# A hybrid decoder block: transposes between column halves in its last stage, and attention's output turned by an fp32 product

## The chip, the cores and the metric

The kernel runs on one core of one Trainium2 chip. The metric is the device time of one execution in microseconds (us). Three runs of the kernel before the change gave 1221.88, 1227.33 and 1224.06 us, with a median of 1224.06 us.

## The reference

One decoder layer on 1024 tokens of 1024 features, all in fp32:

```
hn  = RMSNorm(x)
z   = hn @ w_in                  # q | k | v | forget logits | pool input
A   = causal softmax attention, 8 heads of 64, logits += c[t] - c[s], c = cumsum(log sigmoid(f))
B   = multi-scale causal means of the pool input, minus the token, per-group linear
h   = x + RMSNorm(concat(RMSNorm(A), RMSNorm(B)) @ w_out)
h   = h + RMSNorm(SwiGLU(RMSNorm(h)))        # 1024 -> 2816 -> 1024
out = h + sigmoid(h @ w_ple_gate) * RMSNorm(p @ w_ple_proj)
```

## The kernel before, in words

A product of fp32 precision is made of three products of reduced fp32 (`mm3`, lines 111 to 113): each operand is split into a high part (a cast on ScalarE, line 105) and a low part (a subtraction on VectorE, line 106), and hi·hi, hi·lo and lo·hi are added up in PSUM. Tokens come in 8 tiles of 128, features in 8 blocks of 128. `transposed` (line 121) turns a tile by TensorE transposes against an identity, four to a PSUM bank, and splits what it turned.

The program is written as straight loops, and a planner orders each engine's instructions ahead of time by its own estimate of when each becomes ready, the earlier in the program text the more urgent. Each engine then works through its list strictly in that order; an instruction that waits holds up all behind it. `issue_after(ins)` puts what is written under it behind `ins` on that engine. DMAs are issued from the SP queue, except where named.

The stages: (1) the embedding of p, the norm of x, v and forget logits; (2) the pool mixer, with `pool_in` and `pool_out`; (3) q and k, by `qk_pair`, which for a pair of heads computes q and k as 2 x 2 products of 24 matmuls of 512 columns (`project`), splits each into `qk_hi` (ScalarE, line 409) and `qk_lo` (VectorE, line 410), and writes both to `qd` and `kd` in HBM. `qk_hi` and `qk_lo` have one buffer each; (4) attention, one `head(h)` after another, which reads `qs`, `kh`, `kl`, `vh` and `ncb` back from HBM, and for each of four groups of two query tiles makes scores, softmax (line 439), turned probabilities, and the product with v into bank `O` (lines 469, 470). Since v is held as hi beside lo, that product has 128 rows: 64 from v's high part and 64 from its low part. It is copied to `ot` (line 472), turned by two TensorE transposes (line 475), and the two parts are added: a copy on ScalarE (478), an addition on VectorE (479), and the scaling by 1/sum on GpSimd (480); (5) output projection, SwiGLU and the down projection; (6) the last stage, the gate of the p embedding.

PSUM has 8 banks, dealt out by tags. `psum_layout` deals them anew: before `head(0)`, from A=3, F=2, T=2, O=1 to A=2, T=3, O=2, F=1. `qk_pair(0)` and `qk_pair(1)` use the tags A and F of the old layout in turn, five banks; `qk_pair(2)` and `qk_pair(3)` use F of the new one, a single bank, between the heads' matmuls.

In the last stage, `hidden(t)` loads h1 and the embedding of token tile t (`he`), computes the row norm of `acc` (line 98 on ScalarE, 91 and 93 on GpSimd), scales it (`dn`, line 1002), adds it to h1 (line 1003, on GpSimd for all tiles but the first), and turns and splits it (`h3`, line 121 for all tiles but the first; the first is turned in the down stage, line 1048). `gated(t)` multiplies it with the gate's weights in two halves of 512 columns (banks A and F, 24 matmuls each), applies the sigmoid (line 1066), the product and the sum (1067, 1068), and writes out. `hidden(t + 1)` stands ahead of `gated(t)` in the program.

Of the kernel before, what the change touches and what calls it, by code (L numbers as in the profile page):

```python
# [8 lines left out]
F32 = mybir.dt.float32  # L9
F32R = mybir.dt.float32r  # L10
BF16 = mybir.dt.bfloat16
AF = mybir.ActivationFunctionType
# [24 lines left out]
def block_kernel(ctx: ExitStack, tc: tile.TileContext, x, p, g_mix_pre, w_in, b_forget, g_attn_grp,  # L37
# [8 lines left out]
    def pool(stack, name, bufs=1, side=None):  # L46
        return stack.enter_context(tc.tile_pool(name=name, bufs=bufs, side=side, reuse_waits="tile"))
# [21 lines left out]
    make_identity(nc, ident)  # L69
    identb = const.tile([P, P], BF16, name="identb")  # L70
    nc.vector.tensor_copy(identb, ident)
    maskf = const.tile([P, P], BF16, name="maskf")
    nc.gpsimd.memset(maskf, 0.0)
    nc.gpsimd.affine_select(out=maskf, in_=maskf, compare_op=ALU.is_ge, fill=NEG, base=0,
# [49 lines left out]
    def tok(t):  # L124
        return slice(t * P, (t + 1) * P)
# [317 lines left out]
    def head(h):  # L443
        qs = st.tile([P, S], F32R, name="qs")
        nc.sync.dma_start(out=qs.bitcast(F32), in_=qd[h])
        kh = st.tile([P, S], F32R, name="kh")
        kl = st.tile([P, S], F32R, name="kl")
        for j in range(2):
            nc.sync.dma_start(out=kh[j * DH:(j + 1) * DH, :].bitcast(F32), in_=kd[h][0:DH, :])
            nc.sync.dma_start(out=kl[j * DH:(j + 1) * DH, :].bitcast(F32), in_=kd[h][DH:P, :])  # L450
        vh = st.tile([P, NT, P], F32R, name="vh")
        nc.sync.dma_start(out=vh.bitcast(F32), in_=vd[h])
        ncb = st.tile([P, S], F32, name="ncb")
        nc.sync.dma_start(out=ncb, in_=cd[h:h + 1, :].partition_broadcast(P))
        for g in range(NT // 2):
            nj = 2 * g + 2
            pTs = [pt_.tile([P, NT, W2], F32R, name=f"pT{i}") for i in range(2)]
            rsum = sp.tile([P, 2], F32, name="rsum")
            for qi in range(2):
                i = 2 * g + qi  # L460
                s_sb = scores(h, i, qs, kh, kl, ncb, rsum[:, qi:qi + 1])
                cols = slice(qi * P, (qi + 1) * P)
                transposed(s_sb, pTs[0][:, :, cols], pTs[1][:, :, cols], i + 1, "T")
            rinv = sp.tile([P, 2], F32, name="rinv")
            nc.vector.reciprocal(rinv, rsum)
            po = bank("O")
            for j in range(nj):
                q0 = max(0, j - 2 * g) * P
                nc.tensor.matmul(po[:, q0:W2], vh[:, j, :], pTs[0][:, j, q0:W2], start=j == 0, stop=False)
                nc.tensor.matmul(po[:, q0:W2], vh[:, j, :], pTs[1][:, j, q0:W2], start=False, stop=j == nj - 1)  # L470
            ot = sp.tile([P, W2], F32, name="ot", bufs=2)
            nc.scalar.copy(ot, po[:, 0:W2])
            pr = bank("O")
            for qi in range(2):
                nc.tensor.transpose(pr[:, tok(qi)], ot[:, tok(qi)], ident)
            oh = sp.tile([P, 2, DH], F32, name="oh", bufs=2)
            pv = pr[:, 0:W2].rearrange("a (j x d) -> a j x d", x=2, d=DH)
            nc.scalar.copy(oh, pv[:, :, 0, :])
            nc.vector.tensor_tensor(out=oh, in0=oh, in1=pv[:, :, 1, :], op=ALU.add)
            nc.gpsimd.tensor_tensor(out=a_sb[:, 2 * g:2 * g + 2, h * DH:(h + 1) * DH], in0=oh,  # L480
                                    in1=rinv.unsqueeze(2).broadcast_to([P, 2, DH]), op=ALU.mult)

    qk_pair(0, "AF")
    qk_pair(1, "AF")
    psum_layout(A=2, T=3, O=2, F=1)
    head(0)
    head(1)
    qk_pair(2, "F")
    head(2)
# [10 lines left out]
    def wide(name, dt=F32, shape=(2, D)):  # L500

        return wg.tile([P, *shape], dt, name=name, tag="wide", bufs=2)
# [425 lines left out]
    with ExitStack() as c1:  # L928
        fds = [pool(c1, f"fd{i}", side="right") for i in range(3)]
        acc = pool(c1, "accp").tile([P, NT, D], F32, name="acc")  # L930
        gfp = pool(c1, "gfpp").tile([P, D], F32, name="gfp")
        sgp = pool(c1, "sgp", 6)
        rawp = [pool(c1, f"rawp{i}", 8) for i in range(2)]

# [56 lines left out]
            split(raw, wpg[k][0], wpg[k][1])  # L993

        def hidden(t):
            he = wide("he")
            ht, et = he[:, 0, :], he[:, 1, :]
            nc.sync.dma_start(out=ht, in_=h1d[tok(t), :])
            nc.sync.dma_start(out=et, in_=ed[tok(t), :])
            dn = narrow("dn")  # L1000
            r = row_rstd(acc[:, t, :], D, "y")
            nc.vector.scalar_tensor_tensor(out=dn, in0=acc[:, t, :], scalar=r, in1=gfp, op0=ALU.mult, op1=ALU.mult)  # L1002
            (nc.gpsimd if t else nc.vector).tensor_tensor(out=ht, in0=ht, in1=dn, op=ALU.add)  # L1003
            h3 = [fds[t % 3].tile([P, KT, P], F32R, name=f"h3{i}", tag="lr"[i]) for i in range(2)]
            if t:
                transposed(ht, h3[0], h3[1], KT, "T")
            return ht, et, h3

        LAST = len(steps) - 1
        WPG_AT = {LAST - 13: 0, LAST - 11: 1, LAST - 9: 2, LAST - 8: 3, LAST - 7: 4, LAST - 4: 5, LAST - 3: 6, LAST - 2: 7}  # L1010
# [6 lines left out]
        for j, (ci, i, u) in enumerate(steps):  # L1017
            if j + 2 <= LAST:
                prepare(j + 2)
            if j == LAST // 2:  # L1020
                nc.sync.dma_start(out=gfp, in_=g_ffn_post[0:1, :].partition_broadcast(P))
            if j in WPG_AT:
                with tc.issue_after(last_load[0]):
                    load_wpg(WPG_AT[j])
            name, kind, outs = SUMS[i]
            (l, r), which = made.pop((name, u)), (ci + (kind > 0)) % 2
            fresh, begins, ends = i in (0, 1, 5), u == CHUNKS[ci][0], u == CHUNKS[ci][-1]
            if fresh and begins:
                sets[which] = [down_ps.tile([P, 2, HALF], F32, name=f"dp{which}{x}") for x in range(2)]
            for t in range(4):  # L1030
                pv = sets[which][t // 2]
                for k in range(len(u)):
                    for x, (a_, b_) in enumerate(((0, 0), (0, 1), (1, 0))):
                        nc.tensor.matmul(pv[:, t % 2, :], l[:, a_, k, tok(t)], r[:, b_, k, :],  # L1034
                                         start=fresh and begins and k == 0 and x == 0,
                                         stop=ends and k == len(u) - 1 and x == 2, skip_group_check=not fresh)
                if ends and t % 2 == 1:
                    for sh, dh in outs:
                        av = acc[:, 4 * sh + t - 1:4 * sh + t + 1, half(dh)]
                        if (sh, dh, t) in touched:  # L1040
                            nc.vector.tensor_tensor(out=av, in0=pv, in1=av, op=ALU.add)
                        else:
                            nc.scalar.copy(av, pv)
                            touched.add((sh, dh, t))
                if j == LAST and t == 1:
                    tp = down_ps.tile([P, 2, HALF], F32, name=f"dp{1 - which}0").rearrange("a n (j b) -> a (n j) b", b=P)
                    for c in range(KT):
                        nc.tensor.transpose(tp[:, c, :], prev[0][:, c * P:(c + 1) * P], ident)
                    split(tp, prev[2][0], prev[2][1])
            if j == LAST - 2:  # L1050
                with tc.issue_after(last_load[0]):
                    prev = hidden(0)
# [2 lines left out]
        for tag in "TFOA":  # L1055
            bank(tag)

        def gated(t, ht, et, h3):
            for c0, c1_, tag in ((0, 512, "A"), (512, 1024, "F")) if t < NT - 1 else ((0, 512, "A"), (512, 768, "F"), (768, 1024, "A")):
                cols, n = slice(c0, c1_), c1_ - c0  # L1060
                ps = bank(tag)[:, 0:n]
                for k in range(KT):
                    mm3(ps, (h3[0][:, k, :], h3[1][:, k, :]), (wpg[k][0][:, cols], wpg[k][1][:, cols]),
                        k == 0, k == KT - 1)
                sg = sgp.tile([P, HALF], F32, name="sgm")[:, 0:n]
                nc.scalar.activation(out=sg, in_=ps, func=AF.Sigmoid)  # L1066
                nc.vector.tensor_tensor(out=sg, in0=sg, in1=et[:, cols], op=ALU.mult)  # L1067
                nc.vector.tensor_tensor(out=ht[:, cols], in0=ht[:, cols], in1=sg, op=ALU.add)  # L1068
                nc.sync.dma_start(out=out[tok(t), cols], in_=ht[:, cols])

        for t in range(NT):
            nxt = hidden(t + 1) if t + 1 < NT else None
            gated(t, *prev)
            prev = nxt
    banks["ctx"].close()
    f_ctx.close()

# [25 lines left out]
```

## Time and profile before

| | |
|---|---|
| median of three runs | 1224.06 us |
| the profiled execution: its time, its span | 1219.11 us, 1217.3 us |
| granted TensorE clock, mean | 0.997 |
| PE / DVE / ACT / POOL busy, share of the span | 97% / 61% / 44% / 19% |

PE is TensorE's matmul queue, PEld its weight loads, DVE VectorE, ACT ScalarE, POOL GpSimd, SP the queue that issues DMAs. A busy PE is not a PE at its peak, since a matmul's record runs from start to its modelled end, and neighbours overlap. What sets the pace is the distance from one start to the next.

### The profile page before, as it was taken

Reading aid. Unit: us, or ns where it says so; the run is one execution under the profiler, and the core shown is the slowest. Engines: PE = TensorE matmul, PEld = TensorE weight load, DVE = VectorE, ACT = ScalarE, POOL = GpSimd, SP = SyncE. Lnnn points to the kernel's source line nnn. Section 1 sums busy time; section 2 is a strip of 40 time slices with the busy share of each in tenths; the row PEclk is TensorE's granted clock in tenths of the full one; section 3 lists DMA queues with packets and bytes.
Section 4 is the critical chain, followed back from the end, with each engine's and each line's share of the span. In section 5 each row is a group of like instructions: output and inputs, shape, how many; then the busy total and the mean of one; then the engine's idle time right before and its main releaser. Section 6 shows DMA issues by size and latency. Waiting matters only on the chain. (4 is left out here: it accounts for less than half of the span.)

```text
span 1217.3 us, 15811 instructions
## 1 busy us (share of the span) xinstructions
PE 1181.7 (97%) x5832; PEld 978.4 (80%) x5832; DVE 742.3 (61%) x1129; ACT 538.7 (44%) x990; POOL 229.7 (19%) x277
## 2 busy tenths in 40 slices
PE   8999998999999999899999999999999999998998
PEld 6998887887887887688888888888877888887777
DVE  6544834557775568865555456554576967976323
ACT  6433534557875554633333333334245433544111
POOL 2110110000002530242323233232210000004120
PEclk9999999999999999999999999999999999999999
DMA  9732485549831443232332323323266363442332
GB/s 300 238 105 62 138 241 179 152 122 277 241 89 53 156 141 120 97 111 96 121 113 80 110 96 121 101 82 122 98 221 219 106 240 102 157 168 83 114 137 87
DMA packets 110989, 170.19 MB, mean 140 GB/s; under 512 B 9408, under 2 KB 64512, under 8 KB 110912
## 3 DMA queue, kind: packets, MB, share of 16 engines
q1 hardware_dynamic: 110352, 167.35, 42.3%
q0 software_dynamic: 560, 1.84, 0.4%
q8 instruction: 46, 0.75, 0.2%
q14 instruction: 31, 0.25, 0.1%
HBM read 119.58 MB, written 49.58 MB: 139 GB/s over the span
## 5 line engine op out<-in xcount | busy, mean ns | idle before, releaser
L1034 PE MATMUL dp<-r,l 128*128 128x512 f32 x924 | 211.9, 390 | 3.2 <-DVE l L106 2.5
L1034 PEld LDWEIGHTS dp<-r,l 128*128 128x128 f32 x924 | 172.8, 188 | 41.7 <-DVE l L106 4.7
L621 POOL TENSOR_TENSOR w_raw<-w_raw 128x512 f32<-128x512 f32 x80 | 118.0, 1478 | 285.3 <-DMA w_raw<-in_w_ffn_gate_dram 117.2
L106 DVE TENSOR_TENSOR wr<-w_raw,wr 128x512 fp32r<-128x512 f32 x88 | 65.2, 743 | 72.8 <-ACT wr L105 72.4
L106 DVE TENSOR_TENSOR wl<-w_raw,wl 128x512 fp32r<-128x512 f32 x62 | 55.6, 914 | 47.7 <-ACT wl L105 47.7
L105 ACT CAST wr<-w_raw 128x512 fp32r<-128x512 f32 x88 | 54.4, 620 | 62.9 <-PE ps_O L645 14.5
L105 ACT CAST l<-l 128x1024 fp32r<-128x1024 f32 (+1 forms) x42 | 41.1, 980 | 82.7 <-DMA l<-fa_S 46.5
L645 PE MATMUL ps_F<-T,wr 128*128 128x512 f32 x300 | 73.3, 391 | 1.8 <-ACT wr L105 1.0
L645 PEld LDWEIGHTS ps_F<-T,wr 128*128 128x128 f32 x300 | 56.2, 188 | 14.7 <-ACT wr L105 1.4
L645 PE MATMUL ps_A<-T,wr 128*128 128x512 f32 x264 | 64.3, 390 | 0.0
L106 DVE TENSOR_TENSOR l<-l 128x1024 fp32r<-128x1024 f32 (+1 forms) x42 | 47.4, 1133 | 25.2 <-ACT l L105 25.0
L106 DVE TENSOR_TENSOR pT<-ps_T,pT 128x512 fp32r<-128x512 f32 (+2 forms) x96 | 51.1, 552 | 18.8 <-ACT pT L105 18.1
L645 PE MATMUL ps_O<-T,wr 128*128 128x512 f32 x252 | 62.3, 391 | 0.0
L645 PE MATMUL ps_T<-T,wr 128*128 128x512 f32 x240 | 59.7, 391 | 1.1 <-ACT wr L105 1.1
L645 PEld LDWEIGHTS ps_A<-T,wr 128*128 128x128 f32 x264 | 49.5, 188 | 10.7
L105 ACT CAST wl<-w_raw 128x512 fp32r<-128x512 f32 x62 | 37.0, 619 | 46.9 <-DMA w_raw<-in_w_ffn_gate_dram 11.4
L439 ACT ACTIVATE s_sb<-s_sb,mn 128x128 f32<-128x128 f32 (+3 forms) x64 | 49.9, 781 | 16.1 <-DVE mn L435 15.7
L106 DVE TENSOR_TENSOR r<-B,r 128x1024 fp32r<-128x1024 f32 (+1 forms) x42 | 47.5, 1130 | 15.0 <-ACT r L105 14.9
L645 PEld LDWEIGHTS ps_O<-T,wr 128*128 128x128 f32 x252 | 47.3, 188 | 10.3
L645 PEld LDWEIGHTS ps_T<-T,wr 128*128 128x128 f32 x240 | 45.0, 188 | 11.2 <-ACT wr L105 1.5
L111 PE MATMUL ps_F<-hT,wc_hi 128*128 128x512 f32 x128 | 50.9, 397 | 1.3 <-DVE qk_lo L410 1.3
L113 PE MATMUL ps_F<-hT,wc_lo 128*128 128x512 f32 x128 | 51.0, 398 | 0.0
(317 smaller groups left out, 2767.6 us busy)
## 6 DMA issues: line engine op xcount, KB each, us to landing
w_raw<-in_w_ffn_gate_dram SPq DMA_DIRECT2D x11, 1024.0 KB, 5.6
w_raw<-in_w_ffn_up_dram SPq DMA_DIRECT2D x11, 1024.0 KB, 5.2
fa_S<-lt SPq DMA_DIRECT2D x40, 256.0 KB, 2.1
B<-in_w_ffn_down_dram SPq DMA_DIRECT2D x20, 512.0 KB, 7.7
l<-fa_S SPq DMA_DIRECT2D x20, 512.0 KB, 3.8
xt<-in_x_dram SPq DMA_DIRECT2D x16, 512.0 KB, 4.6
fa_A<-lt SPq DMA_DIRECT2D x30, 256.0 KB, 2.0
l<-fa_A SPq DMA_DIRECT2D x15, 512.0 KB, 3.7
```

Source lines behind the costliest of these rows:

```text
L105: nc.scalar.copy(hi, raw)
L106: lo_by.tensor_tensor(out=lo, in0=raw, in1=hi.bitcast(F32), op=ALU.subtract)
L111: nc.tensor.matmul(ps, lh, rh, start=first, stop=False)
L113: last_pe[0] = nc.tensor.matmul(ps, ll, rh, start=False, stop=last).ins
L439: nc.scalar.activation(out=s_sb[:, 0:nk], in_=s_sb[:, 0:nk], func=AF.Exp, scale=-1.0, bias=mx, accum_out=rsum)
L621: adder.tensor_tensor(out=out, in0=x_, in1=y_, op=op)
L645: last_pe[0] = nc.tensor.matmul(ps, l, r, start=first and k == 0 and i == 0, stop=k == K2 - 1 and i == 2, skip_group_check=not first).ins
L1034: nc.tensor.matmul(pv[:, t % 2, :], l[:, a_, k, tok(t)], r[:, b_, k, :], start=fresh and begins and k == 0 and x == 0, stop=ends and k == ...
```

## The change

Four edits.

- Attention's output: a constant `both` (128 x 64, fp32) is the sum of the identity's left and right half. In place of two transposes of `ot` there are two matmuls with `ot` as the stationary and `both` as the moving operand, in plain fp32, which turn it and add the two parts at once. The copy on ScalarE, the addition on VectorE and the scaling on GpSimd become one multiplication on VectorE that reads PSUM.
- `qk_pair(1)` is moved from ahead of the new PSUM layout to behind `head(0)`, and uses the single bank F.
- Last stage, `hidden`: the addition to h1 is always on VectorE; the turned tile has its own pool `h3p`; `he` has a third buffer in `fds[0]`; the transposes are no longer part of it. `hidden(1)` is issued in the down stage, behind the split of the first tile on VectorE and ScalarE; `hidden(t + 2)` then stands ahead of `gated(t)`.
- Last stage, `gated`: the next tile's transposes and splits stand between the first and the second column half. `sgp` goes from 6 to 3 buffers, and pools change their order.

```diff
+    both = const.tile([P, DH], F32, name="both")
+    nc.vector.tensor_tensor(out=both, in0=ident[:, 0:DH], in1=ident[:, DH:P], op=ALU.add)
...
             for qi in range(2):
-                nc.tensor.transpose(pr[:, tok(qi)], ot[:, tok(qi)], ident)
-            oh = sp.tile([P, 2, DH], F32, name="oh", bufs=2)
-            pv = pr[:, 0:W2].rearrange("a (j x d) -> a j x d", x=2, d=DH)
-            nc.scalar.copy(oh, pv[:, :, 0, :])
-            nc.vector.tensor_tensor(out=oh, in0=oh, in1=pv[:, :, 1, :], op=ALU.add)
-            nc.gpsimd.tensor_tensor(out=a_sb[:, 2 * g:2 * g + 2, h * DH:(h + 1) * DH], in0=oh,
+                nc.tensor.matmul(pr[:, qi * DH:(qi + 1) * DH], ot[:, tok(qi)], both, start=True, stop=True)
+            nc.vector.tensor_tensor(out=a_sb[:, 2 * g:2 * g + 2, h * DH:(h + 1) * DH],
+                                    in0=pr[:, 0:P].rearrange("a (j d) -> a j d", d=DH),
                                     in1=rinv.unsqueeze(2).broadcast_to([P, 2, DH]), op=ALU.mult)
     qk_pair(0, "AF")
-    qk_pair(1, "AF")
     psum_layout(A=2, T=3, O=2, F=1)
     head(0)
+    qk_pair(1, "F")
     head(1)
...
+        h3p = pool(c1, "h3p", 2)
+        rawp = [pool(c1, f"rawp{i}", 8) for i in range(2)]
         gfp = pool(c1, "gfpp").tile([P, D], F32, name="gfp")
-        sgp = pool(c1, "sgp", 6)
-        rawp = [pool(c1, f"rawp{i}", 8) for i in range(2)]
+        sgp = pool(c1, "sgp", 3)
...
         def hidden(t):
-            he = wide("he")
+            he = wide("he") if t % 3 < 2 else fds[0].tile([P, 2, D], F32, name="he", tag="l")
...
-            (nc.gpsimd if t else nc.vector).tensor_tensor(out=ht, in0=ht, in1=dn, op=ALU.add)
-            h3 = [fds[t % 3].tile([P, KT, P], F32R, name=f"h3{i}", tag="lr"[i]) for i in range(2)]
-            if t:
-                transposed(ht, h3[0], h3[1], KT, "T")
-            return ht, et, h3
+            nc.vector.tensor_tensor(out=ht, in0=ht, in1=dn, op=ALU.add)
+            return ht, et, [h3p.tile([P, KT, P], F32R, name=f"h3{i}") for i in range(2)]
...
                     split(tp, prev[2][0], prev[2][1])
+                    with tc.issue_after(last_on(BOTH[0])), tc.issue_after(last_on(BOTH[1])):
+                        nxt = hidden(1)
...
-        def gated(t, ht, et, h3):
+        def gated(t, ht, et, h3, nxt):
...
+                if c0 and nxt:
+                    with tc.issue_after(last_pe[0]):
+                        transposed(nxt[0], nxt[2][0], nxt[2][1], KT, "T")
+                    nxt = None
...
         for t in range(NT):
-            nxt = hidden(t + 1) if t + 1 < NT else None
-            gated(t, *prev)
-            prev = nxt
+            after = hidden(t + 2) if t + 2 < NT else None
+            gated(t, *prev, nxt)
+            prev, nxt = nxt, after
```

## Rows read from the trace of the kernel before

**Rows 1.** The page, busy us of each engine with share and instructions.
```profile
PE 1181.7 (97%) x5832; PEld 978.4 (80%) x5832; DVE 742.3 (61%) x1129; ACT 538.7 (44%) x990; POOL 229.7 (19%) x277
```
**Rows 2.** Waits of PE, whole span: us in total, times, longest.
```profile
PE ps_A L113 <- DVE h L106: 3.4, 1, 3.4
PE ps_O L121 <- DMA pt<-in_p_dram: 3.0, 1, 3.0
...
PE ps_A L111 <- ACT h L105: 1.7, 6, 0.3
```
**Rows 3.** Timeline, start of last stage: start, us, engine, line, operation, [idle before <-releaser].
```profile
1108.67 0.99 ACT L105 CAST h<-dp 128x1024 fp32r<-128x1024 f32 x1
...
1108.96 1.09 PE L121 MATMUL ps_T<-ident,he 128*128 128x128 f32 x8
...
1111.44 1.28 DVE L1002 SCALAR_TENSOR_TENSOR dn<-acc,y_r,gfp 128x1024 f32<-128x1024 f32 x1 [0.72 <-POOL y_r L93]
...
1112.64 1.22 DVE L106 TENSOR_TENSOR h<-dp,h 128x1024 fp32r<-128x1024 f32 x1
...
1113.91 0.80 PE L113 MATMUL ps_A<-wpg,h 128*128 128x512 f32 x1 [3.40 <-DVE h L106]
```
**Rows 4.** Chain that ended last, last stage: start, us, engine, tile, line.
```profile
1120.65 0.24 PE ps_F L111
...
1125.78 0.23 PE ps_F L112
...
1138.62 0.50 PE ps_A L111
...
1201.80 0.50 PE ps_A L111
...
1213.17 0.39 ACT sgm L1066
```
**Rows 5.** Windows: stretch, busy us (instructions) per engine, PEclk, DMA share, GB/s.
```profile
195.00:200.00 5.00, 5.00 (x24) 4.08 (x24) 2.65 (x10) 2.95 (x9) 0.00 (x0) 0.66 0.85 263
...
290.00:392.00 102.00, 96.87 (x640) 80.86 (x639) 74.55 (x213) 75.44 (x190) 11.68 (x27) 1.00 0.50 147
...
1113.00:1126.00 13.00, 12.09 (x46) 9.74 (x47) 5.96 (x7) 5.03 (x8) 1.89 (x5) 0.87 0.06 21
```
**Rows 6.** Timeline, three kinds of weight loads in a row (PEld).
```profile
104.56 0.19 PEld L298 LDWEIGHTS ps_O<-cw,before 64*64 64x64 f32 x2 [0.35 <-issue]
...
168.51 1.87 PEld L394 LDWEIGHTS ps_O<-ones,sq 128*128 128x128 f32 x15
...
1137.06 1.03 PEld L121 LDWEIGHTS ps_T<-ident,he 128*128 128x128 f32 x8
```
**Rows 7.** Groups by line, 198 to 392 us: busy us, mean ns | idle before.
```profile
L480 POOL TENSOR_TENSOR a_sb<-oh,rinv 128x128 f32<-128x128 f32 x32 | 13.3, 415 | 197.2 <-DVE oh L479 196.0 <-DVE rinv L465 1.2
...
L479 DVE TENSOR_TENSOR oh<-oh,ps_O 128x128 f32<-128x128 f32 x32 | 8.9, 277 | 3.5 <-ACT oh L478 3.4
L478 ACT COPY oh<-ps_O 128x128 f32<-128x128 f32 x32 | 8.6, 267 | 7.9 <-PE ps_O L475 7.8
L475 PEld LDWEIGHTS ps_O<-ident,ot 128*128 128x128 f32 x64 | 8.3, 140 | 3.0 <-ACT ot L472 0.7
```
**Rows 8.** Timeline around the second q/k pair.
```profile
168.28 0.39 PE L111 MATMUL ps_F<-hT,wc_hi 128*128 128x512 f32 x1
...
173.53 0.69 DVE L410 SCALAR_TENSOR_TENSOR qk_lo<-ps_A,qk_hi 128x512 fp32r<-128x512 f32 x1 [2.86 <-DMA kd<-qk_lo]
...
189.98 0.60 ACT L409 ACTIVATE qk_hi<-ps_A 128x512 fp32r<-128x512 f32 x1 [13.04 <-DMA qd<-qk_hi]
...
193.92 0.44 PE L429 MATMUL ps_A<-kh,qs 128*128 128x384 f32 x1 [2.46 <-DVE mn L435]
```
**Rows 9.** SP's timeline, and DMA issues from 174.5 us: count, KB, us to landing.
```profile
175.24 0.43 SPq L454 DMA_DIRECT2D ncb<-cd  x1
...
ncb<-cd SPq DMA_DIRECT2D x1, 512.0 KB, 7.7
```

More of the change, by code (lines that the diff above doesn't have):

```diff
@@ L1002, in hidden, with last_on @@
             nc.vector.scalar_tensor_tensor(out=dn, in0=acc[:, t, :], scalar=r, in1=gfp, op0=ALU.mult, op1=ALU.mult)
-            (nc.gpsimd if t else nc.vector).tensor_tensor(out=ht, in0=ht, in1=dn, op=ALU.add)
-            h3 = [fds[t % 3].tile([P, KT, P], F32R, name=f"h3{i}", tag="lr"[i]) for i in range(2)]
-            if t:
-                transposed(ht, h3[0], h3[1], KT, "T")
-            return ht, et, h3
+            nc.vector.tensor_tensor(out=ht, in0=ht, in1=dn, op=ALU.add)
+            return ht, et, [h3p.tile([P, KT, P], F32R, name=f"h3{i}") for i in range(2)]
+        BOTH = (mybir.EngineType.DVE, mybir.EngineType.Activation)
+        def last_on(engine):
+            return next(i for i in reversed(nc.cur_bb.bb.instructions) if i.engine == engine)
         LAST = len(steps) - 1
```

## Prediction

> **What bounds the kernel now.** I read the engines' busy times first, then who made TensorE wait, then three stretches in the timeline: the start of the last stage, the start of attention, and attention itself. The first view [rows 1] shows PE busy for 97% of the span, DVE for 61%, ACT for 44%. PE is the bound almost everywhere, so an instruction taken from another engine is worth nothing by itself; an edit counts by what it adds to PE's work and by the PE idle time that it fills. The list of PE's waits [rows 2] is short: its longest single entry is 3.4 us, PE waiting for the low part of the first turned tile in the last stage.
>
> That wait is worth a look in the timeline [rows 3]. ACT cast the high part by 1108.67 + 0.99 = 1109.66. The subtraction on DVE needs only that, yet it began at 1112.64, 3.0 us later, because in DVE's list it stood behind two scalings of later tiles, and the last of these waited for GpSimd's row norm, itself behind GpSimd's addition for tile 1. PE resumed at 1113.91 after 3.40 us of idling, and the granted clock averaged 0.87 over the next 13 us [rows 5]: the lower level is 0.5 of the higher one, so an average of 0.87 is 3.4 us at 1.2 GHz and costs 0.13 x 13 = 1.7 us.
>
> **The last stage, term by term.** The chain [rows 4] gives the pace: from 1120.65 to 1125.78 are 22 matmuls, 0.233 us each. A token tile has 48, hence 11.2 us. Eight transposes have their weight loads in 1.03 us, one of which lasts 0.14 [rows 6, 7], so 0.89/7 = 0.127 us apart, 1.02 us a tile. Work per tile is 12.2 us. The first matmul of a tile comes at 1138.62 and, five tiles on, at 1201.80: 12.64 us apart. The 0.42 us between is PE waiting for the cast of what it just turned (the six waits of 0.3 in [rows 2]) and the refilling of its weights. That happens at six tile borders, 2.5 us.
>
> After the change hidden(1) stands behind the first split on DVE and ACT, and GpSimd adds no tile, so the subtraction can begin at 1109.66, and the third matmul at 1110.9. From there 46 matmuls take 10.7 us, to 1121.6. Seven tiles of 12.2 us (transposes between the halves, their splits under 5.6 us of the second half) end at 1207.1. Before, the last matmul ended where its sigmoid began, at 1213.17 [rows 4]. **Last stage: -6.0 us.** That is a floor of pure PE work, so the gain can't be larger. The smallest that I can argue for is the wait alone, less the transposes of tile 1, which formerly filled PE ahead of it [rows 3] and now come later: 3.0 - 1.0 = 2.0 us, with the low clock and all bubbles left. I take 6.0, since each part has a named cause and the work that hides it is there: DVE's load per tile becomes 1.28 for the scaling, 1.22 for the addition and, by the 0.69 us of a DVE operation on 512 columns [rows 8], some six of these, 6.6 us of 12.2. The third buffer of he keeps the two loads of tile t+2 a whole tile ahead of their use. Three sigmoid buffers suffice at one half per 5.6 us.
>
> **The product that turns and adds.** Removed per group: two transposes, one ACT copy (0.267), one DVE addition (0.277), one GpSimd product (0.415) [rows 7]; added: two fp32 matmuls and one DVE product of 128 columns from PSUM, which I price like the addition that goes, 0.277. DVE is unchanged; ACT and GpSimd gain 32 x 0.267 = 8.6 and 13.3 us, off PE's path. PE decides. The only plain fp32 product of the kernel, line 298 in the code, stands in the trace as two weight loads, 0.19 us together for 64 columns [rows 6]. Weight loads of 128 columns with almost no matmul behind them, 15 in a row, take 1.87 us, 0.125 each, a little less since the last one's whole length is in it; I take 0.120. So a group costs 4 x 0.120 = 0.48 us in place of 2 x 0.127 = 0.254; with 64 moving columns the loads, not the matmuls, set the pace. That is 0.226 us x 32 groups = 7.2 us more on PE. Bounds: nothing (all of it falls into PE's gaps) and 7.2. Heads 0 to 3 have q and k matmuls to fill every gap, so their 3.6 us stay. In heads 4 to 7 PE idles 102 - 96.9 = 5.1 us [rows 5], waiting on chains that the product doesn't lengthen; I let half of their 3.6 us vanish there. **Product: +5.4 us.** The Trainium skill has a rule that speaks louder against this edit: by "FP8 and Floating Point Precision", section TensorE Precision Notes, true fp32 takes four passes through the array. The trace shows two load and matmul pairs for line 298, and doesn't show what goes on inside a pair; with a load for each of four passes the edit alone would cost 22.6 us (rival 3).
>
> The constant itself is one short DVE instruction, at most 0.28 us by [rows 7], while PE waits 3.0 us for the first p tile [rows 2]: nothing. Without that cover it would cost its 0.28.
>
> **The second q/k pair.** Before, PE ran its four products of 24 matmuls back to back, some 22 us, over the time in which head 0's operands go to HBM and back; five banks held the results, though ACT and DVE could not empty them: they waited for the writes of qk_hi and qk_lo to land, 2.86 us at 173.53 and 13.04 us at 189.98 [rows 8]. Head 0's first softmax stood behind that on both engines, so PE idled 2.46 us at 193.92, and the clock averaged 0.66 from 195 to 200, 0.34 x 5 = 1.7 us. The old order costs 4.2 us.
>
> After, head 0 goes first, but its last operand lands at 175.24 + 7.7 = 182.9 [rows 9], bound by DMA. PE's cover until then is the moved pair, now with one bank. Its first product ends at 168.28 (the second starts there [rows 8]); the bank is free when DVE is done at 173.53 + 0.69 = 174.2. In these 5.9 us PE has 1.9 us of the pool's row sums [rows 6], so 4.0 us are idle; the next product, 24 x 0.23 = 5.5 us, runs to 179.7, and emptying it (0.60 + 0.69 [rows 8]) leaves 1.3 us more before head 0 has anything. With a low clock after it as in [rows 5], 1.7 us, the new order costs 7.0 us there. What queues behind the waiting matmul on PE is all of head 0. Bounds: -4.2 (the old stall goes, and the planner finds cover), and +7.0 (the new stalls come, and the old one stays, since the last two products still meet writes that have not landed). **Taken: 7.0 - 4.2 = +2.8 us**, old stall replaced by new. PE's work in heads 0 to 3 is the same in both orders, so the pair as a filler wins nothing later.
>
> **Sum.** -6.0 + 5.4 + 2.8 = +2.2 us on the profiled execution's 1219.1 (span 1217.3 and 1.8 around it), so 1221.3. The median of the runs shown, 1224.06, lies 5.0 us above that execution, so I predict 1226.3, 1226 us. No change, then: 0.5% of the time is 6.1 us, about what a measurement of this kernel can tell from nothing.
>
> **Rivals.**
> 1. *The product hides and the pair fits* (faster). Speaking for it: ACT and DVE are busy for three quarters of 290 to 392 us [rows 5], so their chains could shorten, and the moved pair gives head 0 a filler that doesn't block ACT. Then product +1.8 and pair -4.2: -6.0 + 1.8 - 4.2 = -8.4, 1215.7; with nothing for the product 1213.9. Against: a full PE has no room in heads 0 to 3. Chance 0.30.
> 2. *One bank starves PE* (slower). Place: 168 to 195 us. Price: new stalls and the old, +7.0, with the product at its full 7.2: +8.2, 1232.3. It decides from the point where PE idles over 6 us more there than before. For it: the DMA waits of [rows 8]; against: the writes of the moved pair come behind the loads of head 0, so they may block less. Chance 0.16.
> 3. *Four loads per product* (slower). 64 x (4 x 0.120 - 0.127) = 22.6: -6.0 + 22.6 + 2.8 = +19.4, 1243.5. The two loads of line 298 speak against it. Chance 0.05.
> 4. *The last stage's edit doesn't do what it says*: the planner believes the next tile late and puts its transposes behind the second half after all. Then -2.0 + 5.4 + 2.8 = +6.2, 1230.3, on the border. Against it, DVE has half of each tile free. Chance 0.08, of which 0.05 over the border.
>
> **Numbers.** The forecast has 0.41; no change is 0.41 + 0.03 = 0.44, faster 0.30, slower 0.16 + 0.05 + 0.05 = 0.26. The range runs from rival 1 with nothing for the product, 1214, to beyond rival 2, 1236, leaving out the four loads and a little on each side. The forecast's own range is 1219 to 1230: the product from 0 to 7.2, the pair 3 us to either side.
>
> **What the profile will show.** The last stage: PE's wait for the subtraction under 1.5 us in place of 3.40, no low clock behind it, tiles 12.2 us apart, and no waits for casts at their borders. Attention: 128 weight loads of `ot` in place of 64, 0.12 us apart, no operation on `oh`. The pair: PE idle near 170 to 174 and 180 us, head 0's softmax before 190 us. I am wrong if weight loads of `ot` cost PE nothing, if PE doesn't stop between the pair's products, or if DVE's order in the last stage again holds a split back.

## The result and the profile after

The changed kernel takes 1229.56 us (median of 14 runs, 1224.96 to 1234.12), the kernel before 1223.54 us beside it (14 runs, 1220.14 to 1227.33): a ratio of 1.0054, 95% interval 1.0042 to 1.0067. That is 0.54% slower, just past the 0.5% that the prediction took as the line between no change and slower, with an interval on both sides of the line. The forecast of 1226.3 us was 3.3 us short; the time lies inside its range and inside the likeliest case's own range of 1219 to 1230. The profiled execution has a span of 1226.1 us, 8.8 more than before; that is more than the 6.0 between the medians, since the profiled execution of the kernel before was a quick one (1219.11 us). One of the four executions of e8, an experiment below, took 2378 us and is left out of its ratio; the other three took 1237.6 to 1237.7.

The page's first part, busy time of each engine:

```profile
PE 1185.5 (97%) x5896; PEld 987.7 (81%) x5896; DVE 750.3 (61%) x1137; ACT 533.6 (44%) x958; POOL 200.7 (16%) x238
```

Beside [rows 1] PE has 64 more loads and matmuls, ACT 32 fewer instructions, GpSimd 39 fewer; the shares of PE, DVE and ACT are the same. What PE waited for (us in total, times, longest) shows where the time went:

```profile
PE ps_A L432 <- DMA kh<-kd: 5.1, 1, 5.1
...
PE ps_A L433 <- DMA kl<-kd: 3.9, 1, 3.9
...
PE ps_A L114 <- ACT h L108: 2.0, 1, 2.0
...
PE ps_O L397 <- DVE sq L109: 1.2, 1, 1.2
```

The 3.4 us for the first split and the six border waits of [rows 2] are gone. In their place stand 9.0 us for the two parts of head 0's keys, which before didn't appear at all, and one border wait of 2.0. (Lines of this kernel are up to 10 higher than before: the cast and subtraction of a split are L108 and L109, the gate's three matmuls L114 to L116, a transpose L124.)

**The stretch of the moved pair**, windows of before and then of after (columns as in [rows 5]):

```profile
160.00:200.00 40.00, 37.54 (x178) 30.84 (x177) 13.22 (x27) 12.59 (x24) 3.88 (x3) 0.96 0.92 279
290.00:390.00 100.00, 94.87 (x632) 79.17 (x631) 73.13 (x212) 75.44 (x190) 10.63 (x26) 1.00 0.51 150
```

```profile
160.00:200.00 40.00, 29.21 (x123) 22.79 (x122) 11.44 (x27) 11.97 (x22) 4.26 (x3) 0.83 0.91 240
...
165.00:170.00 5.00, 4.03 (x23) 3.59 (x24) 2.82 (x4) 0.90 (x2) 1.82 (x2) 0.88 0.83 231
170.00:175.00 5.00, 4.99 (x17) 3.68 (x16) 0.17 (x1) 0.00 (x0) 0.04 (x1) 0.78 1.00 313
175.00:180.00 5.00, 0.00 (x0) 0.00 (x0) 0.69 (x1) 1.88 (x2) 0.00 (x0) 0.91 1.04 218
180.00:185.00 5.00, 1.04 (x4) 0.81 (x5) 0.00 (x0) 0.00 (x0) 0.00 (x0) 0.50 1.03 246
185.00:190.00 5.00, 5.00 (x16) 4.01 (x16) 0.81 (x5) 0.98 (x4) 0.00 (x0) 0.57 1.05 230
...
290.00:390.00 100.00, 97.04 (x662) 84.01 (x660) 72.14 (x211) 69.95 (x165) 0.93 (x4) 1.00 0.54 163
```

From 160 to 200 us PE is busy for 29.2 us in place of 37.5 and issues 123 matmuls in place of 178. Between 175 and 185 it does almost nothing, and the granted clock falls to its lower level, 0.50, and stays there for most of the five busy microseconds after it. From 290 to 390 PE idles 3.0 us of 100 in place of 5.1, but at another part of its work: it is some 15 us behind by then.

The timeline of after for that stretch:

```profile
165.97 1.83 PE L397 MATMUL ps_O<-ones,sq 128*128 128x2 f32 x15 [1.19 <-DVE sq L109]
...
166.97 0.68 DVE L413 SCALAR_TENSOR_TENSOR qk_lo<-ps_F,qk_hi 128x512 fp32r<-128x512 f32 x1
...
167.67 0.48 PE L114 MATMUL ps_F<-hT,wc_hi 128*128 128x512 f32 x1
...
175.03 0.60 ACT L412 ACTIVATE qk_hi<-ps_F 128x512 fp32r<-128x512 f32 x1 [9.13 <-PE ps_F L116]
175.66 0.69 DVE L413 SCALAR_TENSOR_TENSOR qk_lo<-ps_F,qk_hi 128x512 fp32r<-128x512 f32 x1 [5.41 <-ACT qk_hi L412]
180.04 0.77 PE L432 MATMUL ps_A<-kh,qs 128*128 128x128 f32 x2 [5.05 <-DMA kh<-kd]
184.72 0.45 PE L433 MATMUL ps_A<-kl,qs 128*128 128x128 f32 x1 [3.92 <-DMA kl<-kd]
...
185.51 0.78 PE L114 MATMUL ps_F<-hT,wc_hi 128*128 128x512 f32 x1
```

The pair's first product starts at 167.67, right behind the emptying of bank F, which held the last product of the first pair until 166.97 + 0.68 = 167.65. Its own result is out of the bank at 175.66 + 0.69 = 176.35, but the pair's second product (last line) starts at 185.51. In PE's list head 0's first scores stand ahead of it, and they wait for keys that land at 180 and 184.7.

**The last stage.** Timeline of the first tile and of the border to the second one:

```profile
1122.60 1.01 ACT L108 CAST h<-dp 128x1024 fp32r<-128x1024 f32 x1 [8.78 <-PE dp L1052]
...
1123.65 1.23 DVE L109 TENSOR_TENSOR h<-dp,h 128x1024 fp32r<-128x1024 f32 x1 [1.83 <-ACT h L108]
...
1124.93 0.50 PE L116 MATMUL ps_A<-wpg,h 128*128 128x512 f32 x1 [0.27 <-DVE h L109]
...
1132.33 1.03 PE L124 MATMUL ps_T<-ident,he 128*128 128x128 f32 x8
...
1135.01 1.06 ACT L101 ACTIVATE junk<-acc 128x1024 bf16<-128x1024 f32 x1 [1.71 <-POOL y_ms L94]
...
1136.18 1.28 ACT L1076 ACT_TABLE_LOAD   x1
...
1137.97 1.07 ACT L108 CAST h<-ps_T 128x512 fp32r<-128x512 f32 x2
1138.60 0.50 PE L114 MATMUL ps_A<-wpg,h 128*128 128x512 f32 x1 [2.02 <-ACT h L108]
```

The subtraction now begins 0.04 us after the cast ends; [rows 3] had 3 us there. But the split of tile 1, turned at 1132.33, isn't cast before 1137.97: on ACT the squares of later tiles' norms and a table load stand ahead of it. From the third tile on a tile takes 11.79 us, where [rows 4] have 12.64. Two lines of the chain, the eight transposes of tiles two apart, show it, (1204.86 - 1181.28)/2:

```profile
1181.28 0.87 PE ps_T L124 x8
...
1204.86 0.87 PE ps_T L124 x8
```

First gate matmul to last gate matmul takes 97.65 us (1124.03 to 1221.68), before 103.05 (1109.81 to 1212.86): the stage wins 5.4 us. It begins 14.2 us later than in the trace of before. Over it, from 1124 to 1222, the granted clock is 1.00.

### The profile page after: what moved, and what is told of

It is laid out like the page before. It is cut to its first block, busy times and chain, and to the rows that moved or that the text cites. A ratio compares the mean times of both kernels' runs of the same rounds, so it can differ in the third digit from the quotient of the medians.

```text
span 1226.1 us, 15812 instructions
## 1 busy us (share of the span) xinstructions
PE 1185.5 (97%) x5896; PEld 987.7 (81%) x5896; DVE 750.3 (61%) x1137; ACT 533.6 (44%) x958; POOL 200.7 (16%) x238
## 5 line engine op out<-in xcount | busy, mean ns | idle before, releaser
L109 DVE TENSOR_TENSOR wr<-w_raw,wr 128x512 fp32r<-128x512 f32 x88 | 64.7, 736 | 73.4 <-ACT wr L108 73.0
L109 DVE TENSOR_TENSOR wl<-w_raw,wl 128x512 fp32r<-128x512 f32 x62 | 56.3, 926 | 48.6 <-ACT wl L108 48.6
L108 ACT CAST wr<-w_raw 128x512 fp32r<-128x512 f32 x88 | 54.4, 620 | 60.6 <-PE ps_O L645 13.9
L108 ACT CAST l<-l 128x1024 fp32r<-128x1024 f32 (+1 forms) x42 | 41.1, 980 | 82.1 <-DMA l<-fa_S 46.1
L109 DVE TENSOR_TENSOR pT<-ps_T,pT 128x512 fp32r<-128x512 f32 (+2 forms) x96 | 50.8, 551 | 18.6 <-ACT pT L108 18.3
L109 DVE TENSOR_TENSOR l<-l 128x1024 fp32r<-128x1024 f32 (+1 forms) x42 | 47.4, 1133 | 22.1 <-ACT l L108 22.1
L114 PE MATMUL ps_F<-hT,wc_hi 128*128 128x512 f32 x144 | 59.1, 410 | 0.1
L108 ACT CAST wl<-w_raw 128x512 fp32r<-128x512 f32 x62 | 36.9, 619 | 49.9 <-DMA w_raw<-in_w_ffn_gate_dram 13.3
L115 PE MATMUL ps_F<-hT,wc_hi 128*128 128x512 f32 x144 | 58.1, 403 | 0.0
L116 PE MATMUL ps_F<-hT,wc_lo 128*128 128x512 f32 x144 | 58.0, 403 | 0.0
L438 DVE CUSTOM_DVE_ANT_0 s_sb<-ps_A,ncb 128x512 f32<-128x512 f32 (+2 forms) x64 | 37.3, 585 | 33.0 <-PE ps_A L435 17.8
L109 DVE TENSOR_TENSOR r<-B,r 128x1024 fp32r<-128x1024 f32 (+1 forms) x42 | 47.5, 1130 | 15.3 <-ACT r L108 15.2
```

The source lines that it names most:

```text
L108: nc.scalar.copy(hi, raw)
L109: lo_by.tensor_tensor(out=lo, in0=raw, in1=hi.bitcast(F32), op=ALU.subtract)
L114: nc.tensor.matmul(ps, lh, rh, start=first, stop=False)
L115: nc.tensor.matmul(ps, lh, rl, start=False, stop=False)
L116: last_pe[0] = nc.tensor.matmul(ps, ll, rh, start=False, stop=last).ins
L438: nc.vector.tensor_tensor_reduce(out=s_sb[:, c0:c1_], in0=ps[:, 0:n], in1=ncb[:, c0:c1_], scale=-1.0, scalar=3.0e38 if mx is None else mx, ...
```

## Experiments

Ratios are against the kernel before, run beside each; "us" are differences of medians.

### Each of the three edits alone

**e1_last_stage**: the changed kernel with the old product and the old order, so the last stage's edits alone.

```diff
-                nc.tensor.matmul(pr[:, qi * DH:(qi + 1) * DH], ot[:, tok(qi)], both, start=True, stop=True)
+                nc.tensor.transpose(pr[:, tok(qi)], ot[:, tok(qi)], ident)
...
+    qk_pair(1, "AF")
     psum_layout(A=2, T=3, O=2, F=1)
     head(0)
-    qk_pair(1, "F")
```

> The last stage's edits alone, on the kernel before. Theory (three separate terms that add up: last stage -6, product about +5, moved pair about +7): 1217.5 us, ratio 0.995. Rival (the gain seen at the end of the trace of after is only time that the stages ahead lost and that is caught up there): no change, 1223.5.

**e2_product**: the kernel before with `both` and the product, nothing else (the first hunk of e1, the other way round).

> The fp32 product alone, on the kernel before. Theory: +5 us, 1229, ratio 1.004, nearly all of it as 128 weight loads 0.11 us apart in place of 64. Rival A (the product carries most of the loss, since the groups behind it start late): +11 us, 1234.5. Rival B (the loads fall into PE's gaps): within 2 us of before.

**e3_pair**: the kernel before with the second hunk alone, the other way round: the pair behind head 0.

> The moved q/k pair alone, on the kernel before. Theory: +7 us, 1230.5, ratio 1.006, with PE waiting some 9 us for kh and kl between 173 and 186 us and a low clock behind it. Rival A (the product carries the loss): +1 us, 1224.5. Rival B (later gaps in attention are filled by the pair and give it back): no change.

**e4_pair_back**: the changed kernel with the pair put back, so last stage and product together.

> The changed kernel with the pair's move undone (last stage and product stay). Theory: 1229.6 - 7 = 1222.5 us, the same as before. Rival A (product carries the loss): 1228.5.

Measured:

| kernel | median us | ratio, interval | us | predicted term |
|---|---|---|---|---|
| e1, last stage | 1216.88 | 0.9945, 0.9928 to 0.9962 | -6.5 | -6.0 |
| e2, product | 1225.13 | 1.0016, 1.0003 to 1.0029 | +1.8 | +5.4 |
| e3, pair | 1235.95 | 1.0108, 1.0087 to 1.0130 | +12.6 | +2.8 |
| e4, last stage and product | 1220.34 | 0.9968, 0.9953 to 0.9983 | -3.0 | -0.6 |

The three alone add up to +7.9, the change measured +6.0; intervals of 2 to 3 us on each leave room for that. So the last stage's term holds in sum, the product costs a third of what was priced (its interval allows 0.4 to 3.5 us), and the pair costs more than the upper bound of 7.0. Against the expectations, e1 came out; e2 fell to its rival B, within 2 us of before; e3 cost 5.6 us more than its theory, and e4 was 2.2 us faster. Without the moved pair the change would have been a gain.

e3's trace shows the pair's loss without the other edits:

```profile
160.00:200.00 40.00, 31.32 (x133) 24.82 (x131) 11.44 (x27) 11.94 (x23) 4.26 (x3) 0.83 0.92 251
300.00:360.00 60.00, 53.57 (x338) 43.57 (x337) 42.62 (x120) 43.35 (x106) 3.93 (x10) 1.00 0.77 227
```

PE is idle 8.7 us from 160 to 200 (before 2.5), at 0.83 of the clock in place of 0.96, and 6.4 us from 300 to 360, where the kernel before idles 2.5 (2.7 at the same part of its work, 281 to 341).

### Why the pair costs so much

**e8_one_bank**: the kernel before, the pair still ahead of head 0, but with its products in the one bank F.

```diff
-    qk_pair(1, "AF")
     psum_layout(A=2, T=3, O=2, F=1)
+    qk_pair(1, "F")
     head(0)
```

> The kernel before with the new PSUM layout ahead of qk_pair(1), so that the pair has the single bank F, but stays ahead of head 0. Theory (what the moved pair loses is PE standing at head 0's scores, planned too early, not the bank): within 3 us of before, no wait of PE for kh or kl. Rival (one bank starves PE, as predicted): +9 us or more, 1232, with PE idle between the pair's products.

Measured: 1237.69 us, ratio 1.0116 (1.0097 to 1.0134), +14.2 us. Its theory, that the bank doesn't matter, is refuted: with one bank the loss is there in the old order too, so that at one bank the place in the written order is not what decides. The trace says why the two are alike. The written order is only an input to the planner, and PE's list in e8 comes out as after the move, with head 0's scores ahead of the pair's second product:

```profile
178.27 0.77 PE L429 MATMUL ps_A<-kh,qs 128*128 128x128 f32 x2 [4.02 <-DMA kh<-kd]
...
183.01 0.45 PE L430 MATMUL ps_A<-kl,qs 128*128 128x128 f32 x1 [3.97 <-DMA kl<-kd]
```

**e11_two_banks** and **e12_banks_control**: two banks F and two T for attention, with the pair moved and with the pair in its old place.

```diff
-    psum_layout(A=2, T=3, O=2, F=1)
+    psum_layout(A=2, T=2, O=2, F=2)
```

> The moved pair alone, as in the run that costs 12.6 us, but with two banks F for the products of attention and two banks T in place of three. Theory (one bank F between the pair's products starves TensorE, so that head 0's scores overtake the second product): the second product goes straight behind the first, TensorE idles under 5 us between 160 and 200 us in place of 8.7, the granted clock there is over 0.93, and the time is within 3 us of its control with the same banks and the pair in its old place. Rival (the move itself costs, since head 0's loads and the pair's writes or the casts compete whatever the banks): still over 8 us slower than the control.

> The kernel before with two banks F and two banks T in place of one and three for the attention stage, the pair in its old place: control for the run with two banks. Both theories: within 4 us of before, either way; the last two pairs gain from a second bank F, the turning of the probabilities loses a bank T.

Measured: e11 1234.32 us, ratio 1.0098 (1.0078 to 1.0118), +10.9 us; e12 1225.95 us, ratio 1.0023 (1.0006 to 1.0040), +2.6 us. So e11 is 8.4 us slower than its control, with some 3 us of uncertainty: not within 3 us, as the theory of the bank asked, but over 8, as its rival did (the move itself costs, whatever the banks). The comparison doesn't part the two, though. In e12 the pair stands ahead of the new layout and still has the old one's five banks, so e11 differs from it in place and in banks. A pair ahead of head 0 with two banks was not run. Windows of e11:

```profile
160.00:200.00 40.00, 34.42 (x163) 27.57 (x161) 10.29 (x22) 12.14 (x22) 4.26 (x3) 0.96 0.93 258
```

and in its timeline

```profile
180.29 0.46 PE L429 MATMUL ps_A<-kh,qs 128*128 128x128 f32 x2 [2.27 <-DMA kh<-kd]
...
184.92 0.30 PE L430 MATMUL ps_A<-kl,qs 128*128 128x128 f32 x1 [1.45 <-DMA kl<-kd]
...
294.84 0.80 PE L111 MATMUL ps_F<-wob,mt 128*128 128x512 f32 x1 [5.61 <-ACT wob L105]
```

With a second bank the second product does run between the scores: in 160 to 200 PE idles 5.6 us in place of e3's 8.7 (under 5 was expected; its control 1.6), and the clock stays at 0.96. Idle time and low clock together, about half of the local loss goes. Of what is left there, 3.7 us are the wait for the keys (first two lines). Part of the gain is then lost at 294.84, where PE stands 5.61 us at a product of the output projection whose weights aren't cast yet; in the control that wait is 3.50. Other traces have the same wait. In those of e3 and e8 it is, in total, times and longest,

```profile
PE ps_F L111 <- ACT wob L105: 3.4, 3, 2.2
...
PE ps_F L111 <- ACT wob L105: 3.6, 2, 2.9
```

and in the changed kernel PE waits 2.1 us for those weights' DMA. With the pair in its old place and three banks T the waits for them come to 0 to 1.7 us in nine traces. So this stall comes with the pair that runs late, and two banks T alone bring it too (e12, 3.8 in total). Why the weights are late isn't shown.

### Does the product's price hide in gaps?

**e9_product_twice**: e2 with each product issued twice into the same place.

```diff
-                nc.tensor.matmul(pr[:, qi * DH:(qi + 1) * DH], ot[:, tok(qi)], both, start=True, stop=True)
+                for _ in range(2):
+                    nc.tensor.matmul(pr[:, qi * DH:(qi + 1) * DH], ot[:, tok(qi)], both, start=True, stop=True)
```

> The product edit alone, with each fp32 product issued twice, so a dose of 64 more fp32 products (128 weight loads, 14.3 us at 0.112 each). The first dose cost 1.8 us for 7.3 us of added loads. Theory (the first dose went into gaps that TensorE had between the chains of attention, and these are filled now): the second dose costs 9 us or more, so about 1235 to 1239, and TensorE's idle time in attention doesn't shrink further. Rival (the loads run under matmuls of other products and cost nothing in themselves): the second dose costs about twice the first's 1.8, some 2 to 5 us, so 1228 to 1230.

Measured: 1241.31 us, ratio 1.0167 (1.0136 to 1.0198), +17.9 us. The second dose costs 17.9 - 1.8 = 16.1 us, with some 4 us of uncertainty, for 128 added loads of 0.112 = 14.3 us: full price. The first dose, 64 loads more, 7.2 us by the same count, cost 1.8.

The theory had the first dose fall into gaps. Three groups in the timelines, of before, e2 and e9, each with the matmul behind it, show that PE pays for it on the spot:

```profile
285.36 0.38 PE L475 MATMUL ps_O<-ident,ot 128*128 128x128 f32 x2
285.49 0.36 PE L469 MATMUL ps_O<-pT,vh 128*128 128x256 f32 x1
```

```profile
290.72 0.55 PE L478 MATMUL ps_O<-both,ot 128*128 128x64 f32 x4
291.08 0.37 PE L472 MATMUL ps_O<-pT,vh 128*128 128x256 f32 x1
```

```profile
225.49 1.00 PE L479 MATMUL ps_O<-both,ot 128*128 128x64 f32 x8
226.30 0.36 PE L472 MATMUL ps_O<-pT,vh 128*128 128x256 f32 x1
```

From a group's first matmul to the next instruction are 0.13 us before, 0.36 in e2 and 0.81 in e9; these are also about the medians of all 32 groups. So 0.23 us a group, 7.4 us in all, is added in e2, and some 5.6 us come back elsewhere. In part the traces show where: the distances from start to start of the product with v add up to 41.5 us in e2 (41.0 to 41.8 in e4, e9 and the changed kernel), against 43.8 to 45.0 in the six traces with the old product and the old order (before, e1, e5, e6, e7, e13), those of the scores to 40.7 against 41.8 to 42.3. PE's idle time proper, from the first q/k matmul to the end of the output projection, hardly changes: 9.6 us in e2 and 9.5 in e9, 9.2 to 11.8 in those six. (A matmul's record, 0.39 us for 512 columns, outlasts the 0.23 to the next start, so waits under some 0.16 us don't count as idle.) Two readings remain. PE, which is later, may find short waits shorter, which the second dose then finds used up; or the chain behind the product, shorter by an operation on ScalarE and one on GpSimd, may release PE's next work earlier. No run separates them; one with the two transposes and a shorter chain behind them would.

### What the last stage's gain is made of

**e6_vector_add**: the kernel before, addition of each tile's norm on VectorE.

```diff
-            (nc.gpsimd if t else nc.vector).tensor_tensor(out=ht, in0=ht, in1=dn, op=ALU.add)
+            nc.vector.tensor_tensor(out=ht, in0=ht, in1=dn, op=ALU.add)
```

> The kernel before with one word changed: the addition to h1 is on VectorE for all tiles. Theory (place of the turned tile sets the pace): matmuls stay 0.234 us apart in the last stage, and the gain is only what GpSimd's queue cost at the first tile, 1221 to 1223. Rival (GpSimd sets the pace): 0.227 us, 1219 or less.

**e5_gpsimd_add**: e1 with that one line the other way round.

> The last stage's edits alone (1216.9 us) with the addition to h1 back on GpSimd for all tiles but the first. Theory (the stage's matmuls went from 0.234 to 0.227 us because the turned tile now lies in a pool of its own): pace stays 0.227, tiles 11.8 us apart, about 1217. Rival (GpSimd's additions slowed the matmuls): pace 0.234, tiles about 12.1 us apart, 1219.5.

**e13_tile_place**: the kernel before with the turned tile in a pool of its own, as after; transposes, norms and additions as before.

```diff
-        sgp = pool(c1, "sgp", 6)
+        h3p = pool(c1, "h3p", 2)
...
+        sgp = pool(c1, "sgp", 3)
...
-            h3 = [fds[t % 3].tile([P, KT, P], F32R, name=f"h3{i}", tag="lr"[i]) for i in range(2)]
+            h3 = [h3p.tile([P, KT, P], F32R, name=f"h3{i}") for i in range(2)]
```

> The kernel before with one edit: the two halves of the turned tile of the last stage come from their own pool of two buffers, as in the kernel after, and sigm has three buffers; transposes, row norms and GpSimd's addition stay where they were. Theory (the pace of the last stage's 512-column matmuls, 0.234 us before and 0.227 after, follows the place of the turned tile): pace 0.227, first gate matmuls of the tiles 12.3 us apart in place of 12.63, and 2 to 3 us faster than before, ratio about 0.998. Rival (the pace follows the order of the work, transposes between the halves and norms two tiles ahead): pace 0.234, tiles 12.63 apart, no change within 1 us.

**e7_norm_behind_split**: e1 with the norm of tile t+2 issued behind the split of tile t+1 on VectorE and ScalarE, as the change does it for tile 1 alone.

```diff
                         transposed(nxt[0], nxt[2][0], nxt[2][1], KT, "T")
                     nxt = None
+                    if t + 2 < NT:
+                        with tc.issue_after(last_on(BOTH[0])), tc.issue_after(last_on(BOTH[1])):
+                            after.append(hidden(t + 2))
...
-            after = hidden(t + 2) if t + 2 < NT else None
+            after = []
             gated(t, *prev, nxt)
-            prev, nxt = nxt, after
+            prev, nxt = nxt, after[0] if after else None
```

> The last stage's edits alone, with hidden(t+2) issued behind the split of tile t+1 on VectorE and ScalarE. Theory (PE's 2.0 and 0.8 us of waiting at the first border are the squares of tiles 2 to 6, queued ahead of tile 1's cast on ScalarE): those waits go, 1216.9 - 3 = 1214, ratio 0.992. Rival (tile 1's cast is late for another reason, the sigmoid's table load): gain under 1.3 us.

Measured, with the distances from one tile's first gate matmul to the next tile's, in the timelines:

| kernel | median us | ratio, interval | first, second, later distances, us |
|---|---|---|---|
| before | 1223.5 | 1 | 16.28, 12.53, 12.63 |
| e1 | 1216.88 | 0.9945, 0.9928 to 0.9962 | 14.57, 13.08, 11.79 |
| e5 | 1218.65 | 0.9957, 0.9941 to 0.9972 | 14.22, 16.58, 11.79 |
| e6 | 1219.61 | 0.9962, 0.9947 to 0.9977 | 11.29, 12.53, 12.63 |
| e7 | 1212.65 | 0.9909, 0.9891 to 0.9927 | 12.38, 11.78, 11.79 |
| e13 | 1221.86 | 0.9979, 0.9963 to 0.9995 | 16.29, 12.21, 12.3 to 13.0 |

e6 shows that the addition's engine alone makes most of the early stall: with one line the time falls by 4.0 us (0.5 to 2.5 were expected), and in the trace only the first distance shrinks, by 5.0. e5 puts the addition back and keeps the later distances; its loss against e1 stands in the second distance and is too small for the times to confirm. e13 changes the later distances without touching the order of work. Two tile starts of e13, 12.35 apart, each with the border wait that before has:

```profile
1181.08 0.50 PE L111 MATMUL ps_A<-wpg,h 128*128 128x512 f32 x1 [0.29 <-ACT h L105]
...
1193.43 0.50 PE L111 MATMUL ps_A<-wpg,h 128*128 128x512 f32 x1 [0.29 <-ACT h L105]
```

e7 is 11.0 us faster than before and the fastest kernel of the study, 4.2 us faster than e1. Its border to the second tile:

```profile
1119.68 1.07 ACT L105 CAST h<-ps_T 128x512 fp32r<-128x512 f32 x2 [1.20 <-PE ps_T L121]
...
1120.64 1.07 ACT L98 ACTIVATE junk<-acc 128x1024 bf16<-128x1024 f32 x1
...
1124.03 0.39 PE L111 MATMUL ps_A<-wpg,h 128*128 128x512 f32 x1
```

The cast runs while the transposes do, the square comes behind it, and the next tile's first matmul has no idle time ahead of it. In the changed kernel the same matmul waited 2.02 us. The cause of that border's stall, norms of later tiles ahead of the cast, is shown by this run.

## Why the prediction was near, and where it failed

The total came out near by luck: two terms were off in opposite ways, by -3.6 and +9.8 us.

**Last stage, -6.0: right in sum (-6.5), other parts.** The split at the cast's heels, the clock at 1.00 behind it, and no waits at later borders were all as predicted. Two parts were off in size. A new stall wasn't foreseen: the first two distances were to shrink by some 4 us and 0.3 us, and shrank by 1.7 and grew by 0.55, since the norms of later tiles moved from VectorE's list ahead of the subtraction to ScalarE's ahead of the next cast. Against that, later tiles take 11.79 us, where the floor of 12.2 was made of the old pace, 0.233 us for a matmul; the new pace is 0.227, and over 48 matmuls that is 0.3 us of the 0.4 a tile. The prediction called its 6.0 a floor of pure PE work that couldn't be beaten; e7, at -11.0, beats it.

**Product, +5.4: price of a group right, net wrong (+1.8).** The trace of after has 128 loads of `ot` for 64 products, two to a product:

```profile
L478 PEld LDWEIGHTS ps_O<-both,ot x128: 187/192/201, 203.9 to 402.1; 128*128 128x128 f32 x128
L478 PE MATMUL ps_O<-both,ot x128: 217/275/275, 204.1 to 402.2; 128*128 128x64 f32 x128
```

In their groups of four they start 0.112 us apart (predicted 0.120), and a group holds PE 0.23 us longer than two transposes did (predicted 0.226; both sides of that difference were too high, 0.48 for 0.36 and 0.254 for 0.13). The step that failed is what comes back: "Heads 0 to 3 have q and k matmuls to fill every gap, so their 3.6 us stay", and half of heads 4 to 7. One quarter of the 7.2 us was to vanish, three quarters did. The prediction put the relief of ScalarE and GpSimd "off PE's path" and at nothing; whether it is this relief or PE's short waits that gave the time back stays open. Rival 3, four loads to a product, is refuted. The Trainium skill, "FP8 and Floating Point Precision", section TensorE Precision Notes, counts four passes for true fp32. The trace shows two load and matmul pairs, and e9's second dose costs 0.25 us for a product of two loads; whatever passes there are inside a pair, the price here is that of two loads.

**Pair, +2.8: the step that failed.** The prediction had the pair's first product end at 168.28, as in the old order. With one bank it could only start at 167.67, when the last product of the first pair was out of bank F, and it ended some 7 us late. Then the prediction went on: "the next product, 24 x 0.23 = 5.5 us, runs to 179.7". It did not run there. PE's list put head 0's scores first, and their keys weren't there, so that the bank's emptying at 176.35 bought nothing until 185.51. Predicted were 5.3 us of new idle time less the old 2.46; measured were 10.8 in place of 2.5. The clock was to cost 1.7 us as before; its lower level lasted into 185 to 190, and weighing each window's busy time by its clock the loss is some 4.3 us (0.12 of 4.03, 0.22 of 4.99, 0.50 of 1.04 and 0.43 of 5.00), before 0.04 x 37.5 = 1.5. Together 8.3 + 2.8 = 11.1 us in this stretch, where the changed kernel pays 9.2 for the pair (after less e4), so some 2 us came back later. In e3, at 12.6 us, less is lost here and more from 300 to 360. That one bank is enough for the loss, e8 shows; that a second bank takes it away, e11 doesn't bear out.

The Trainium skill, "PSUM — Partial Sum Buffer", section Engine vs sequencer instructions, says that matmuls start and complete in program order. The trace agrees: the pair's second product, whose bank was free at 176.35, stood behind scores that waited until 184.72.

**Rivals.** Rival 2 came true in its first half, past its own point of decision (8.3 us more idle, over 6): one bank starves PE, though by way of scores that wait for their keys, not by writes that have not landed. Its time of 1232.3 wasn't reached: the product cost 5.4 us less than it assumed, the pair 2.2 more. Rival 1 was half right, the product is nearly free in sum; rival 4 is refuted by the transposes at 1132.33, inside the tile.

**The list of signs.** PE's wait for the subtraction 0.27 (under 1.5 expected); no low clock behind it; tiles 11.79 apart (12.2); later borders without waits, the first one with 2.0; PE idle at 175 to 184.7 (170 to 174 and 180); head 0's first softmax at 186.17 (before 190). Of the three signs of being wrong, two stayed away; the third came in small: at 1140.64 PE waited 0.83 us for a low part that stood behind a later tile's scaling in DVE's list (1138.71).

## What to carry to other kernels

When work is moved to cover a wait, look at what the moved work itself needs, its banks here, and at what the in-order list will put ahead of it: a filler with one buffer stops at its own emptying, and whatever comes next in the list stands there in its place. Issue later tiles' preparation behind the cast that the next tile needs, on each engine, not on one. And when a change adds work to one engine and takes it from others, measure the added work on the spot, from its first start to the next instruction's, beside the change's net cost: doubling it showed a price (16.1 us for two loads a product) that the net cost of 1.8 us did not.

## What the runs showed that was not expected

**The pace of the gate's matmuls depends on where tiles lie.** With the turned tile, their stationary operand, in the pools of the factors, the mean distance of 512-column matmuls in the last stage is 0.233 us (before, e2, e3, e6, e8); with it in a pool of its own it is 0.227 to 0.228 (after, e1, e4, e5, e7, e13). The q and k matmuls keep 0.227 in all of them. e13 changes only pools and is 2.2 us faster (ratio 0.9979, 0.9963 to 0.9995); 8 tiles of 48 matmuls at 0.006 us would give 2.3. In its trace the stage itself is only 0.8 us shorter, 102.28 for 103.05, since one distance grew to 13.02, so the link from pace to time rests on the other tiles' distances. The pools' new order also moved the sigmoid's tiles and the pools that hold the gate's weights, the moving operand of the same matmuls. Which of these places matters, and why, stays open.

**The planner's list makes one bank as dear in either order**: +12.6 us with the pair behind head 0, +14.2 ahead of it.
